# A two-layer hybrid block on one core: two modulation chunks change engine and place, and the rotation is written in half as many products

## The chip, the cores and the metric

The kernel runs on one core of one Trainium2 chip. The metric is device time in microseconds (us) of one execution. The engines are named as in the profile: PE (TensorE, matmuls), DVE (VectorE), ACT (ScalarE), POOL (GpSimd) and SP (SyncE, whose queue issues most transfers).

## What is computed

Two layers over 512 latent tokens and 256 context tokens, width 1024, all in fp32. The parts of the reference that matter here are the modulation vectors, which scale, shift and gate each layer, and the rotation of queries and keys by their grid position:

```python
mod   = (silu(c)     @ mod_w[i] + mod_b[i])     # 6 * 1024 values for the latent tokens
mod_c = (silu(c_ctx) @ mod_w[i] + mod_b[i])     # the same for the context tokens
sh_m, sc_m, g_m, sh_f, sc_f, g_f = split(mod, 6)
h  = rms_norm(x, norm_attn_w[i]) * (1 + sc_m) + sh_m
...                                             # three groups of heads, each its own mixer
x  = x + g_m * (concat([ya, yb, yg]) @ w_out[i])
hf = rms_norm(x, norm_ffn_w[i]) * (1 + sc_f) + sh_f
x  = x + g_f * swiglu(hf, ...)
...
def rotate(xh, pos):                            # on each half of a head, for q and k
    x1, x2 = split(xh, 2)
    return xh * cos + concat([-x2, x1]) * sin
```

## The kernel before

Each fp32 product is made of three passes on PE: weights and activations are split into a high and a low part (`wh`, `wl` for weights), and high x high, high x low and low x high are accumulated. So every weight is loaded into a buffer of the tag `wr` (two buffers), copied to `wh` by ACT (L336) and subtracted to `wl` by DVE (L337). `load_wo` loads a quarter-megabyte piece of the output projection in this way.

The 6 x 1024 modulation values of a layer are made in 12 chunks of 512 weight columns, numbered c = 0 to 11. A chunk is four steps of the generator `mod_dots` (L220); a step takes 128 output columns and multiplies the 1024 x 128 weights, laid out with the columns on the partitions, by the two conditioning rows. These stand in four tiles of 128x512 made by `mod_rows` (L206): two of tag `XFB`, one `YO`, one `HD`, each loaded, passed through tanh on ACT (L214), combined on DVE (L215) and scaled on ACT (L216). A step has four dot products of length 512 in each partition. There are two ways to do them. With `aside` true, each half of the weights is loaded into a slot of tag `QN` (L232, 256 KB), GpSimd multiplies (L239) and ScalarE accumulates (L240). With `aside` false, one load of 512 KB goes into a `wr` buffer (L227) and VectorE multiplies and accumulates in one instruction (L242, listed as CUSTOM_DVE in the profile and as ISA by the compiled program). `step_md(n)` advances the running generator by n steps.

In the first layer, chunks 4 to 9 are made beside the input projections, the convolution of the state-space heads and the start of the attention (about 70 to 264 us), all with `aside`. Chunks 10 and 11 of that layer and all twelve of the next are made with VectorE beside the first layer's feed-forward part, at about 540 to 1070 us. Chunks 4 and 5 are the gate of the attention part's residual (used by `residual`, L1149), 8 and 9 are the scale of the feed-forward norm, first used after the output projection (`sc2`).

The convolution runs in blocks of 128 channels on DVE (L773, L780) and ACT (L768, L778) between PE's projections, and its results are transposed by PE (L796). The scan's decay rows come in by loads named `crow` (L908), and are combined on ACT (L913) and DVE (L917). The rotation is in `head_out` (L672): GpSimd makes x * cos, VectorE makes the swapped halves times sin in eight products of 128x64 (L696), then adds them (L697).

The output projection of the first layer runs as 16 blocks: in the loop over `dA` the first four head tiles for each of eight output pieces (blocks 0 to 7), in a second loop the other four for six pieces (8 to 13), and in its tail for the last two. Each block is one `load_wo`, 24 matmuls (`proj_ws`), and a `residual` on DVE. The code gives only the data flow: a scheduler that works ahead of time with a model of durations writes the order of instructions of every engine and queue, and the tile pools assign buffers in that order. An engine runs its list strictly in that order, waiting where it must; so does SP's queue.

## Time and profile before

| | us |
|---|---|
| three runs | 1818.57, 1820.86, 1827.93 |
| median | 1820.86 |
| the profiled execution, its own time | 1828.21 |
| its span | 1826.4 |

The profiled execution is 7.35 us above the median of the runs. The profile's times are microseconds from the start of the span, unless marked ns. PE is busy for 95% of the span, DVE for 58%, ACT for 37%, POOL for 22%; PEclk is the granted clock of TensorE as a share of full speed, whose two levels are 1.2 and 2.4 GHz. In a row of a timeline, the bracket at the end is the time that the engine sat idle before the instruction and what ended that.

### The profile page before, as it was taken

The numbers are of one execution on the slowest core, as the hardware profiler recorded it, in microseconds if no ns is written. First come the engines' busy times: TensorE is split into PE (matmuls) and PEld (weight loads), VectorE is DVE, ScalarE is ACT, GpSimd is POOL, SyncE is SP. The second block draws the span as 40 slices with busy tenths as digits, with TensorE's granted clock in tenths as the row PEclk, the third lists the DMA queues.
The fourth block names the chain that finished last, engine by engine and source line by source line (L and its number), as shares of the span: only waits on it lengthen the run. The fifth ranks groups of instructions, "written<-read, shape, count | busy, mean of one in ns | idle before, by whom it ended". The sixth has DMA issues, their size and how long they took to land.

```text
span 1826.4 us, 26611 instructions
## 1 busy us (share of the span) xinstructions
PE 1733.7 (95%) x10146; PEld 1475.2 (81%) x10146; DVE 1066.0 (58%) x2165; ACT 682.7 (37%) x1376; POOL 399.6 (22%) x429
## 2 busy tenths in 40 slices
PE   7998897899999999999999989998899999999998
PEld 3887785777878888888888878987777888888887
DVE  4659776886575455445554575576686743333334
ACT  4655664556253211121122234334555532222222
POOL 0398875643020000000000010421552100000000
PEclk9999998999989999999999999999899999999999
DMA  9643655422224343333344455233522333333332
GB/s 363 218 145 112 203 153 150 121 87 67 64 70 127 116 126 108 123 103 109 124 118 120 124 159 186 82 115 110 151 72 65 99 93 92 104 93 94 102 106 79
DMA packets 94319, 221.66 MB, mean 121 GB/s; under 512 B 18416, under 2 KB 26224, under 8 KB 94192
## 3 DMA queue, kind: packets, MB, share of 16 engines
q1 hardware_dynamic: 78096, 204.65, 36.6%
q10 hardware_dynamic: 16096, 15.31, 2.5%
q8 instruction: 80, 1.31, 0.3%
q14 instruction: 47, 0.39, 0.1%
HBM read 198.49 MB, written 21.43 MB: 120 GB/s over the span
## 4 chain that ended last, share of the span: by engine, by line
PE 77%; DVE 9%; DMA 6%; ACT 4%; issue 2%; POOL 2%; SPq 0%; ACTq 0%; DVEq 0%; POOLq 0%
PE S L348 60%; PE sm L446 3%; DMA wl<-crow 2%; PE PT L434 2%; PE PT L348 1%; PE PT L362 1%; PE sm L362 1%; DMA wr<-in_mod_wT_dram 1%; PE S L400 1%; PE sm L938 1%; PE sm L939 1%; PE PT L983 1%; DVE MB L773 1%; PE PT L996 1%; DVE wl L337 1%
## 5 line engine op out<-in xcount | busy, mean ns | idle before, releaser
L336 ACT ACTIVATE wh<-wr 128x1024 fp32r<-128x1024 f32 (+2 forms) x204 | 198.0, 972 | 723.8 <-PE S L348 550.7
L337 DVE TENSOR_TENSOR wl<-wr,wh 128x1024 fp32r<-128x1024 f32 (+2 forms) x204 | 231.2, 1134 | 178.9 <-ACT wh L336 177.0
L280 POOL TENSOR_TENSOR tiny<-tiny,mhalf 128x2 f32<-128x2 f32 (+2 forms) x17 | 28.7, 1689 | 1066.4 <-DVE tiny L1195 1018.7
L348 PE MATMUL S<-HY,wh 128*128 128x512 f32 (+1 forms) x716 | 215.8, 359 | 5.6 <-ACT HY L329 4.0
L348 PE MATMUL S<-HZ,wh 128*128 128x512 f32 (+1 forms) x716 | 213.4, 356 | 1.0 <-DVE HZ L330 1.0
L348 PE MATMUL S<-HS,wh 128*128 128x512 f32 (+1 forms) x716 | 213.0, 355 | 0.0
L348 PE MATMUL S<-HY,wl 128*128 128x512 f32 (+1 forms) x716 | 212.8, 355 | 0.1
L348 PE MATMUL S<-HS,wl 128*128 128x512 f32 (+1 forms) x716 | 209.7, 351 | 0.0
L242 DVE CUSTOM_DVE_ANT_0 PT<-wr,XFB 128x512 f32<-128x512 f32 x112 | 75.6, 716 | 185.6 <-DMA wr<-in_mod_wT_dram 185.5
L348 PEld LDWEIGHTS S<-HY,wh 128*128 128x128 f32 x716 | 118.6, 191 | 24.5 <-ACT HY L329 4.2
L348 PEld LDWEIGHTS S<-HZ,wh 128*128 128x128 f32 x716 | 119.5, 192 | 23.0 <-DVE HZ L330 2.8
L348 PEld LDWEIGHTS S<-HY,wl 128*128 128x128 f32 x716 | 118.8, 192 | 19.5 <-DVE wl L337 0.4
L348 PEld LDWEIGHTS S<-HS,wh 128*128 128x128 f32 x716 | 117.9, 190 | 18.2
L348 PEld LDWEIGHTS S<-HS,wl 128*128 128x128 f32 x716 | 116.6, 189 | 19.0
L348 PE MATMUL S<-PHA,wh 128*128 128x512 f32 (+1 forms) x358 | 105.8, 353 | 0.0
L348 PE MATMUL S<-PHB,wh 128*128 128x512 f32 (+1 forms) x358 | 104.5, 350 | 0.0
L348 PE MATMUL S<-GX,wh 128*128 128x512 f32 (+1 forms) x400 | 97.7, 350 | 0.4 <-DVE KA L1149 0.4
L425 POOL TENSOR_SCALAR pr<-pr,tiny 128x640 f32<-128x640 f32 (+2 forms) x80 | 67.8, 851 | 90.3 <-DVE tiny L424 66.1
L239 POOL TENSOR_TENSOR KA<-QN,XFB 128x512 f32<-128x512 f32 x48 | 68.5, 1430 | 40.8 <-ACT XFB L216 23.1
L434 PE MATMUL PT<-c,pr 128*128 128x128 f32 x384 | 65.0, 286 | 12.8 <-POOL pr L425 5.7
L1296 DVE TENSOR_TENSOR MB<-S,MA 128x768 f32<-128x768 f32 (+1 forms) x42 | 34.6, 823 | 70.7 <-PE S L348 70.7
L348 PEld LDWEIGHTS S<-GX,wh 128*128 128x128 f32 x400 | 65.9, 189 | 11.3 <-DVE KA L1149 0.8
(432 smaller groups left out, 3901.2 us busy)
## 6 DMA issues: line engine op xcount, KB each, us to landing
wr<-in_mod_wT_dram SPq DMA_DIRECT2D x56, 512.0 KB, 3.9
wr<-in_w_gate_dram SPq DMA_DIRECT2D x44, 512.0 KB, 3.6
wr<-in_w_up_dram SPq DMA_DIRECT2D x44, 512.0 KB, 3.6
wr<-in_w_blk_dram SPq DMA_DIRECT2D x28, 512.0 KB, 3.8
wr<-in_w_down_dram SPq DMA_DIRECT2D x32, 448.0 KB, 3.4
QN<-in_mod_wT_dram SPq DMA_DIRECT2D x48, 256.0 KB, 3.0
wr<-in_w_out_dram SPq DMA_DIRECT2D x32, 256.0 KB, 2.7
wr<-in_w_down_dram SPq DMA_DIRECT2D x16, 512.0 KB, 3.5
```

The costliest lines, as they stand in the source:

```text
L239: G.tensor_tensor(out=p_, in0=wv, in1=x, op=ALU.mult)
L242: V.tensor_tensor_reduce(out=p_, in0=wv, in1=x, scale=1.0, scalar=0.0, op0=ALU.mult, op1=ALU.add, accum_out=acc[:, o : o + 1],)
L280: POW.tensor_tensor(out=y, in0=v, in1=mhalf[:, 0:n], op=ALU.pow)
L336: S.activation(hi, raw, AF.Copy)
L337: V.tensor_tensor(lo, raw, hi.bitcast(F32), ALU.subtract)
L348: ins = PE.matmul(pt[:, c0:c1], lhsT=w, rhs=xx[:, c0:c1], start=(k == (0 if len(order) == 1 else order[0]) and i == 0), stop=(k == (nk - 1 ...
L362: PE.matmul(pt[:, 0:n], lhsT=s, rhs=w[:, o : o + n], start=(k == 0 and i == 0), stop=(k == KB - 1 and i == 2),)
L400: PE.matmul(st[:, o0:512], lhsT=Q[:, q0 : q0 + P], rhs=K[:, xk[0] : xk[1]], start=(i == 0), stop=(i == 1))
L425: G.tensor_scalar(out=p_, in0=p_, scalar1=m[:, 4:5], scalar2=1.0, op0=ALU.mult, op1=ALU.mult)
L434: PE.transpose(pt[:, k * P : (k + 1) * P], pr[j, qi][:, kk * P : (kk + 1) * P], ident)
L446: PE.matmul(pv[64 * j : 64 * j + 64, 0:P], lhsT=V2(kts[k], j), rhs=ph[j, qi][:, k, :], start=(k == 0), stop=(k == nkt - 1), tile_position= ...
L1296: V.tensor_tensor(gg[:, c0:c1], pu[:, c0:c1], sg[:, c0:c1], ALU.mult)
```

## The change

Chunks 8 and 9 leave the generator of the first layer's early part. They are made instead with `aside` false in the output projection of that layer: `mod_rows` is called there at the first block, and a step is taken after each of the blocks 2 to 7 of the first loop and each of the first two of the second loop: eight steps. The `mod_rows` at the start of the feed-forward part goes; it uses the same four tiles. The rows are all loaded through the two buffers of tag `MA` instead of `MA` and `MB` in turn, and the sums of a chunk get a tile of their own (`macc`, one buffer). The rotation does the two heads of a tile in one product: four products of 128x128 in place of eight of 128x64.

```diff
@@ -209,7 +209,7 @@
         r = []
         for i, tag in enumerate(("XFB", "XFB", "YO", "HD")):
             t = T(sb, tag, BUFS[tag], [P, 512])
-            x = (ma, mb)[i % 2]([P, 512])
+            x = ma([P, 512])
             nc.sync.dma_start(x, a["cvec"][:, i * 512 : i * 512 + 512].to_broadcast([P, 512]))
             S.activation(t, x, AF.Tanh, scale=0.5)
             V.scalar_tensor_tensor(t, t, 1.0, x, ALU.add, ALU.mult)
@@ -219,7 +219,7 @@
 
     def mod_dots(l, c, rows, ptile, aside):
 
-        acc = tiny(16)
+        acc = T(sb, "macc", 1, [P, 16])
         for b in range(4):
             src = a["mod_wT"][l, 4 * c + b]
             if not aside:
@@ -559,7 +559,7 @@
             rows = mod_rows()
             md = (
                 0
-                for c in range(4, 10)
+                for c in range(4, 8)
                 for _ in mod_dots(
                     0, c, rows, lambda: slot("KA")[:, 0:512], True
                 )
@@ -688,12 +688,11 @@
                     in1=cb, op=ALU.mult,
                 )
             sv = sinT.rearrange("p t (f s c) -> p t f s c", f=2, s=2)
-            for h in range(2):
-                x5 = raw[:, 0:4, 64 * h : 64 * h + 64].rearrange("p t (f s c) -> p t f s c", f=2, s=2)
-                o5 = s[:, :, 64 * h : 64 * h + 64].rearrange("p t (f s c) -> p t f s c", f=2, s=2)
-                for f in range(2):
-                    for k in range(2):
-                        V.tensor_tensor(o5[:, :, f, k, :], x5[:, :, f, 1 - k, :], sv[:, :, f, k, :], ALU.mult)
+            x6, o6 = (z.rearrange("p t (h f s c) -> p t h f s c", f=2, s=2, c=16) for z in (raw[:, 0:4, :], s))
+            for f in range(2):
+                for k in range(2):
+                    sb4 = sv[:, :, f, k, :].unsqueeze(2).to_broadcast([P, 4, 2, 16])
+                    V.tensor_tensor(o6[:, :, :, f, k, :], x6[:, :, :, f, 1 - k, :], sb4, ALU.mult)
             V.tensor_tensor(c, c, s, ALU.add)
             rb = r[:, 12 * i : 12 * i + 12].rearrange("p (t h) -> p t h", h=2).unsqueeze(3)
             V.tensor_tensor(v4(raw[:, 0:4, :]), v4(c), rb[:, 0:4].to_broadcast([P, 4, 2, 64]), ALU.mult)
@@ -1217,10 +1216,14 @@
 
         for i, d in enumerate(dA):
             events(nu + i)
+            if not last and i == 0:
+                rows = mod_rows()
+                md = (0 for c in (8, 9) for _ in mod_dots(0, c, rows, ps_t, False))
             w = load_wo(d, 0)
             pt = ps_s()
             proj_ws(pt, w[0], w[1], [yh[k] for k in WK[0:4]], [yl[k] for k in WK[0:4]], 4, osegs)
             residual(d, pt, 2, parts(ntok), False)
+            step_md(int(i > 1))
             events(nu + i + 0.5)
         events(1e9)
         ysh, ysl_ = [yh[k] for k in WK[4:8]], [yl[k] for k in WK[4:8]]
@@ -1229,6 +1232,9 @@
             pt = ps_s()
             proj_ws(pt, w[0], w[1], ysh, ysl_, 4, osegs)
             residual(d, pt, 2, parts(ntok), True)
+            step_md(1)
+        for _ in md:
+            pass
         sc2 = scale_tiles(l, 4, nfw[l])
         hs2 = []
 
@@ -1262,7 +1268,6 @@
         fw = []
         md = iter(())
         if not last:
-            rows = mod_rows()
             md = (
                 0
                 for z in [(0, 10), (0, 11)] + [(1, c) for c in range(12)]
```

Since lines move by one, L1149 of before is L1148 of after, L780 is L779, and so on. The order of instructions changes at these places.

DVE in the output projection, before: `QN`, `KB` with L1149 are residuals of blocks (S is the block's accumulator), L337 makes the low part `wl` of a later block's weights.

```order
L1149 SCALAR_TENSOR_TENSOR KB_902_4416<-S_1051_5005,mod0_4_732,KB_902_4416 128x512
L337 TENSOR_TENSOR wl_1070_5129<-wr_1068_5126,wh_1069_5128 128x512
...
L1149 SCALAR_TENSOR_TENSOR QN_904_4418<-S_1059_5052,mod0_5_857,QN_904_4418 128x512
L337 TENSOR_TENSOR wl_1074_5162<-wr_1072_5159,wh_1073_5161 128x512
...
L1149 SCALAR_TENSOR_TENSOR QN_905_4419<-S_1067_5099,mod0_5_857,QN_905_4419 128x512
L337 TENSOR_TENSOR wl_1078_5195<-wr_1076_5192,wh_1077_5194 128x512
```

After, on DVE at the same place: PT<-wr with `macc` and L242 is the first dot product of a step, the row with HD its last. The first row is the residual of block 3; `wl_1051` belongs to block 4, whose residual has S_1052, and `wl_1058` to block 5.

```order
L1148 SCALAR_TENSOR_TENSOR QN_871_4287<-S_1045_5000,mod0_5_857,QN_871_4287 128x512
...
L242 ISA PT_1036_4974,macc_1034_4971<-wr_1035_4972,XFB_1006_4820 128x512
...
L242 ISA wr_1035_4972,macc_1034_4971<-wr_1035_4972,HD_1012_4838 128x512
...
L242 ISA PT_1047_5029,macc_1034_4971<-wr_1046_5027,XFB_1006_4820 128x512
...
L242 ISA wr_1046_5027,macc_1034_4971<-wr_1046_5027,HD_1012_4838 128x512
...
L337 TENSOR_TENSOR wl_1051_5038<-wr_1049_5035,wh_1050_5037 128x512
L242 ISA PT_1054_5070,macc_1034_4971<-wr_1053_5068,XFB_1006_4820 128x512
...
L242 ISA wr_1053_5068,macc_1034_4971<-wr_1053_5068,HD_1012_4838 128x512
...
L337 TENSOR_TENSOR wl_1058_5079<-wr_1056_5076,wh_1057_5078 128x512
L1148 SCALAR_TENSOR_TENSOR KA_867_4283<-S_1052_5041,mod0_4_732,KA_867_4283 128x512
```

Before, the `wl` of block 4 (`wl_1070`) stood behind the residual of block 1; after, `wl_1051` stands behind the residual of block 3 and two steps of dot products, and from there on each `wl` stands behind one more step. The pattern goes on up to the eighth step, behind which stands the `wl` of block 10.

SP's queue in the output projection, before:

```order
L334 DMA wr_1080_5225<-in_w_out_dram 128x512
L334 DMA wr_1084_5258<-in_w_out_dram 128x512
L334 DMA wr_1089_5293<-in_w_out_dram 128x512
L334 DMA wr_1094_5329<-in_w_out_dram 128x512
L334 DMA wr_1099_5365<-in_w_out_dram 128x512
L334 DMA wr_1104_5401<-in_w_out_dram 128x512
```

After:

```order
L227 DMA wr_1046_5027<-in_mod_wT_dram 128x1024
L334 DMA wr_1049_5035<-in_w_out_dram 128x512
L227 DMA wr_1053_5068<-in_mod_wT_dram 128x1024
L334 DMA wr_1056_5076<-in_w_out_dram 128x512
L227 DMA wr_1060_5109<-in_mod_wT_dram 128x1024
L334 DMA wr_1063_5120<-in_w_out_dram 128x512
L227 DMA wr_1068_5154<-in_mod_wT_dram 128x1024
L334 DMA wr_1071_5162<-in_w_out_dram 128x512
```

Loads of weights followed each other; now each is followed by a load of a modulation step. Both take the tag `wr` and its two buffers: by the addresses, all steps from the second on go to one of them and all weights from block 4 on to the other, the first step's buffer being that of the weights of block 4.

DVE at the first convolution block, before (L780 is the part of the gate on which PE's transposes wait, L282 to L285 the square root's steps, L699 and L701 the rotated heads):

```order
L282 SCALAR_TENSOR_TENSOR tiny36_372_1748<-tiny36_371_1746 128x36
L283 TENSOR_TENSOR tiny36_372_1748<-tiny36_372_1748,tiny36_370_1744 128x36
L285 SCALAR_TENSOR_TENSOR tiny36_373_1751<-tiny36_372_1748,tiny36_371_1746 128x36
...
L699 TENSOR_TENSOR GR_282_1206<-pr_381_1853,tiny36_373_1751 128x512
L701 TENSOR_TENSOR GR_282_1206<-GR_282_1206,tiny36_373_1751 128x256
L701 TENSOR_TENSOR GR_283_1207<-GR_283_1207,tiny36_373_1751 128x256
L701 TENSOR_TENSOR GR_284_1208<-GR_284_1208,tiny36_373_1751 128x256
L780 SCALAR_TENSOR_TENSOR MB_378_1809<-S_377_1759,MB_378_1809 128x512
```

After:

```order
L282 SCALAR_TENSOR_TENSOR tiny36_338_1628<-tiny36_337_1626 128x36
L779 SCALAR_TENSOR_TENSOR MB_344_1689<-S_343_1639,MB_344_1689 128x512
L283 TENSOR_TENSOR tiny36_338_1628<-tiny36_338_1628,tiny36_336_1624 128x36
...
L285 SCALAR_TENSOR_TENSOR tiny36_339_1631<-tiny36_338_1628,tiny36_337_1626 128x36
...
L698 TENSOR_TENSOR GR_282_1206<-pr_347_1733,tiny36_339_1631 128x512
L700 TENSOR_TENSOR GR_282_1206<-GR_282_1206,tiny36_339_1631 128x256
L698 TENSOR_TENSOR GR_283_1207<-pr_360_1885,tiny36_339_1631 128x512
```

L779 of after (L780 of before) has moved ahead of the norms and the rotated heads. On POOL the last L239 is instruction 105 of its list instead of 143, and on SP's queue the eight steps' 16 loads into `QN` ahead of the attention's `nq` and `crow` loads are gone.

## Rows read from the trace of the kernel before

**Rows 1.** The page, part 1: busy us of each engine, share, instructions.

```profile
PE 1733.7 (95%) x10146; PEld 1475.2 (81%) x10146; DVE 1066.0 (58%) x2165; ACT 682.7 (37%) x1376; POOL 399.6 (22%) x429
```

**Rows 2.** Windows: busy us (xcount) of PE, PEld, DVE, ACT, POOL; PEclk, DMA share, GB/s.

```profile
160.00:170.00 10.00, 5.64 (x48) 5.44 (x46) 9.90 (x12) 2.69 (x7) 9.34 (x8) 0.93 0.30 99
...
190.00:200.00 10.00, 5.14 (x27) 4.40 (x27) 8.85 (x13) 4.91 (x13) 5.79 (x5) 0.80 0.17 52
...
260.00:270.00 10.00, 7.57 (x36) 6.38 (x36) 5.63 (x11) 3.76 (x10) 4.32 (x6) 0.83 0.99 237
...
270.00:280.00 10.00, 5.62 (x38) 5.06 (x36) 7.63 (x18) 6.04 (x15) 7.14 (x12) 0.89 0.74 229
...
280.00:290.00 10.00, 6.30 (x25) 4.61 (x24) 8.23 (x23) 3.64 (x10) 3.11 (x3) 0.59 0.34 100
...
470.00:480.00 10.00, 10.00 (x59) 8.73 (x58) 4.81 (x9) 1.77 (x3) 0.00 (x0) 1.00 0.18 53
```

**Rows 3.** Timeline of PE (start, us, engine line op, [idle before <-releaser]).

```profile
170.72 0.90 PE L796 MATMUL PT<-c,MB 128*128 128x128 f32 x3 [5.08 <-DVE MB L780]
...
198.27 0.90 PE L796 MATMUL PT<-c,MB 128*128 128x128 f32 x3 [4.86 <-DVE zt L815]
...
278.64 0.69 PE L400 MATMUL S<-KA,QN 128*128 128x384 f32 x1 [4.38 <-ACT pr L420]
```

**Rows 4.** Instruction groups by line, 60 to 440 us, shapes apart.

```profile
L239 POOL TENSOR_TENSOR KA<-QN,XFB 128x512 f32<-128x512 f32 x48 | 68.5, 1430 | 40.8 <-ACT XFB L216 23.1 <-DMA QN<-in_mod_wT_dram 7.6 <-ACT KA L240 6.3
...
L240 ACT ACTIVATE KA<-KA 128x512 f32<-128x512 f32 x48 | 30.2, 629 | 8.0 <-POOL KA L239 6.8 <-DVE zt L815 0.6 <-ACT QN L240 0.4
...
L696 DVE TENSOR_TENSOR pr<-GR,c 128x64 f32<-128x64 f32 x24 | 15.1, 694 | 3.3 <-DMA gq<-pr 3.0 <-POOL GR L680 0.3
```

**Rows 5.** Timeline of DVE beside the convolution.

```profile
153.62 1.23 DVE L696 TENSOR_TENSOR pr<-GR,c 128x64 f32<-128x64 f32 x8
...
166.85 3.21 DVE L701 TENSOR_TENSOR GR<-GR,tiny 128x256 f32<-128x256 f32 x3
...
185.63 7.37 DVE L696 TENSOR_TENSOR pr<-GR,c 128x64 f32<-128x64 f32 x8 [2.98 <-DMA gq<-pr]
...
210.00 1.25 DVE L248 TENSOR_TENSOR tiny<-tiny 128x8 f32<-128x8 f32 x1
...
244.25 8.55 DVE L917 SCALAR_TENSOR_TENSOR wh<-wh,dtr,wl 128x128 f32<-128x128 f32 x2
...
264.03 0.31 DVE L248 TENSOR_TENSOR tiny<-tiny 128x8 f32<-128x8 f32 x1
```

**Rows 6.** Timeline of POOL: the end of the 64th L239.

```profile
204.95 1.28 POOL L239 TENSOR_TENSOR QN<-QN,HD 128x512 f32<-128x512 f32 x1
```

**Rows 7.** Timeline of SP's queue: issue, with the time that it stood.

```profile
243.14 12.74 SPq L232 DMA_DIRECT2D QN<-in_mod_wT_dram  x3
...
263.45 0.54 SPq L908 DMA_DIRECT2D wl<-crow  x1
```

**Rows 8.** Timeline of ACT: the decay rows of the scan.

```profile
276.54 1.28 ACT L913 ACTIVATE wl<-wl,dtr 128x128 f32<-128x128 f32 x4 [2.27 <-DMA wl<-crow]
```

**Rows 9.** Timeline of DVE in the output projection.

```profile
461.15 1.14 DVE L1149 SCALAR_TENSOR_TENSOR QN<-S,mod,QN 128x512 f32<-128x512 f32 x2 [0.77 <-PE S L348]
...
465.98 1.14 DVE L1149 SCALAR_TENSOR_TENSOR KA<-S,mod,KA 128x512 f32<-128x512 f32 x2 [0.42 <-PE S L348]
...
470.23 1.14 DVE L1149 SCALAR_TENSOR_TENSOR KB<-S,mod,KB 128x512 f32<-128x512 f32 x2 [2.51 <-PE S L348]
```

**Rows 10.** Source L242 (duration ns min/median/max) and source L227 (its loads).

```profile
L242 DVE CUSTOM_DVE_ANT_0 PT<-wr,XFB x112: 691/702/734, 553.0 to 1066.7; 128x512 f32<-128x512 f32 x112
...
DMA to landing us min/median/max: 3.4/3.9/4.8
```

**Rows 11.** PE timeline at 86 us; DMA issues 60 to 110 us.

```profile
86.49 0.76 PE L348 MATMUL S<-HY,wh 128*128 128x512 f32 x2 [1.33 <-DVE MB L294]
...
MA<-in_cvec_dram SPq DMA_DIRECT2D x2, 256.0 KB, 6.0
```

## The prediction

> **What bounds the kernel now.** I first read the busy time of the engines: PE 95%, DVE 58%, ACT 37%, POOL 22% [rows 1]. Then I read windows of 10 us for where PE is not busy. In the output projection PE has 10.00 of 10 us, DVE 4.81, ACT 1.77 and POOL nothing [rows 2]. PE alone is the bound there, and what is added to the other engines is free until it makes PE wait. Beside the convolution it is the other way round: PE has 5.64 of 10 us at 160 to 170 us with DVE at 9.90 and POOL at 9.34, 5.14 at 190 to 200, and 7.57, 5.62 and 6.30 in the three windows from 260 to 290 [rows 2]. Together 19.7 us of these five windows are idle on PE, and the granted clock is below full in all of them (0.93, 0.80, 0.83, 0.89, 0.59, a mean over the two levels 1.2 and 2.4 GHz). So the change takes work from a stage where the side engines set the pace and puts work into one where PE sets it. Third, I read what ended PE's long idle times: a convolution instruction of DVE (5.08 and 4.86 us) and an exponential of ACT (4.38 us) [rows 3].
>
> **What it takes away beside the convolution.** Two chunks are 32 products of 1.43 us on POOL and 32 accumulations of 0.63 us on ACT [rows 4], with 16 loads on SP's queue. POOL and ACT are not the bound by themselves. What matters is whom they hold up, in three places.
>
> *160 to 170 us.* DVE did its rotated heads, three of them in 3.21 us [rows 5], before the L780 for which PE sat idle 5.08 us [rows 3]. In the order after, that instruction stands before them (and before L283 and L285). Of the 4.36 us that PE lacks in this window I take 3: DVE is busy for 9.90 us in any case, so what is passed must be done soon after, before the next convolution block. Bounds 1 and 4.4.
>
> *190 to 200 us.* Eight products L696 took 7.37 us while POOL multiplied, and eight took 1.23 us at 153.62, when it did not [rows 5]. The delay goes with the number of instructions and not with their size: L248, with eight elements in a partition, took 1.25 us at 210.00 and 0.31 at 264.03 [rows 5]. Four products in place of eight should then take half, 3.7 us less, out of a gap of 4.86 us on PE [rows 3]. Bounds: nothing if the delay goes with size, 4.9 if they meet less of POOL.
>
> *250 to 290 us.* With 64 products instead of 96, POOL has done its last one at about 206 us [rows 6]; the last third ran from there to 263 us. Two L917 took 8.55 us at 244.25 beside them [rows 5], at 128 elements each. SP's queue stood for 12.74 us at 243.14 with loads for these products, and the loads of the decay rows (263.45) were behind that [rows 7]; ACT waited 2.27 us for the last of these at 276.54 [rows 8], ahead of the exponential that ended PE's 4.38 us [rows 3]. PE lacks 10.5 us in 260 to 290 [rows 2]. All of these waits fall away, but the chain through decay rows, scores and softmax stays and will now be the late one. I take 9. Bounds: 4.7 (the 2.27 and the 2.4 that PE lacks at 260 to 270), 10.5.
>
> The Trainium skill bears on this ("SBUF — State Buffer", section "SBUF: two separate sides"): VectorE with two inputs from SBUF and GpSimd take one port pair by an exclusive lock, and the loser is blocked for one whole instruction of the other. By that rule two L917 would lose at most two products. The row says more than that (8.55 us, six products long), so the trace agrees that they exclude each other and not on how long; this sum goes by the row.
>
> The clock: in a window with mean clock x, a share 2(1 - x) ran at the lower level, and half of the matmul time there is what it cost. That is 0.4, 1.0, 1.3, 0.6 and 2.6 us in the five windows, 5.9 in all. With the gaps shorter I take 2 of it back (0 to 4). Sum for this stage: 3 + 3.7 + 9 + 2 = 17.7 us less (bounds 6 and 24). In the second layer the rotation meets no POOL products and DVE is off the path: nothing.
>
> **What it adds in the output projection.** A step is four L242 of about 0.70 us [rows 10], 2.6 us with the sums' readout. PE's period for a block is 4.25 us (465.98 to 470.23), and DVE waits for PE 2.51 us in each [rows 9]. By busy time alone DVE would have 0.7 (`wl`, priced as L242 of the same size) + 1.14 (residual) + 2.6 = 4.4 us per 4.25 us block: nearly free. But a step also waits for its load, and the order puts the `wl` of a block behind it. The load takes 3.4 to 4.8 us, median 3.9 [rows 10], and it can't start before the step before it has released the buffer, since all steps from the second on share one.
>
> Let T be the end of block 3 on PE (461.15 in the trace before [rows 9]). DVE then does the residual (1.14), two evictions of y (L297, priced as the residual: 1.14), and step one until T + 4.8; two more L297 until T + 5.9; step two until T + 8.5; then `wl` of block 4 until T + 9.2. PE starts block 4 on its `wh` and needs `wl` 0.7 us later, so it starts at T + 8.4 where it would have started at T + 0.7, after six transposes of y: 7.7 us late. From here step, load and step follow each other. The third step's load starts at T + 8.5. I take 3.7 us for it, between the shortest and the median, since the traffic here is less than in the feed-forward part, where these were measured. It is done at T + 14.8, and block 5 starts at about T + 14.7 instead of T + 4.9: 9.8 us late. Each further step costs 3.7 + 2.6 = 6.3 us against a block of 4.25, 2.05 us more, five times, up to block 10: 20.1 us. The first long gap and those of about 2 us after it will lower the clock, but PE has slack against the loads until the last of them: 1 us. So 21 us more. With a landing of 3.4 us it is 18.3 + 0 = 18.3, with 4.8 it is 26.6. Bounds 18 and 27.
>
> **Smaller things.** `mod_rows` in the tail of the attention is eight ACT instructions like L240 of 0.63 us [rows 4] and four on DVE like L242: 5.0 and 2.8 us, between other work, and on SP's queue the load of block 3's weights stands behind the rows' loads, which wait for `MA`: 1 us taken (0 to 7.8). The same work taken from the feed-forward start lay under a full PE: 0. At the start the third conditioning row must now wait for the first to be used, as both use `MA`, and such a load takes 6.0 us [rows 11]; the write-back L293 then stands behind it on ACT, and PE already waits 1.33 us for its buffer at 86.49 [rows 11]. I take 2 us (0 to 6).
>
> **Sum.** 1828.2 - 17.7 + 21 + 1 + 2 = 1834.5 us for an execution like the profiled one. That one was 7.35 us above the median of the runs shown, so I set the time at 1827.
>
> **Rivals.** *The loads are hidden.* If the steps find their weights ready, DVE's 4.4 us against 4.25 costs 2 us in all, and the gain stays: 1827 - 21 + 2 = 1808 us. For it: before, loads were issued as soon as a buffer was free, and DMA is busy only a fifth of the time here [rows 2]. Against it: one buffer serves all steps, and landing alone is almost a block long. It decides if landing were below 4.25 - 2.6 = 1.7 us, half of the shortest seen.
>
> *The convolution gives little back, and the stall comes* (the slower side). PE's waits at 250 to 290 us may belong to the chain of the attention itself, with DVE at 8.23 of 10 us in 280 to 290 [rows 2] after POOL's products had ended. Then only the lower bound, 6, is gained: 1827 + 11.7 = 1839 us. For it: 3.7 us are missing in 280 to 290, 17 us and more after the last product. Against it: SP's 12.74 us of standing, which delayed all of that. It decides when the gain is below 12.
>
> *One lock per instruction.* If VectorE loses one GpSimd product per instruction, the two L917 lost 2.9 and not 8 us by it, something else held the rest, and the third place gives 4 instead of 9: 1832 us. The L917 row speaks against it.
>
> **Chances and range.** 0.5% is 9.1 us, about what a measurement of this kernel can tell from no change, so the bounds of "same" are 1811.8 and 1830.0. Forecast 0.58, its own range 1814 to 1840; loads hidden 0.14; little gain 0.23; one lock 0.05. Faster: 0.12 of the hidden case and 0.02 of the forecast: 0.14. Slower: 0.21 of little gain, 0.03 of the lock and 0.13 of the forecast, whose centre is only 3 us below the bound: 0.37. Same: 0.49. The range from 1808 to 1842 leaves out the better half of the hidden case and the worse part of little gain, together under 0.2.
>
> **What would show it.** In the profile after: PE idle for about 8 us before block 4 of the output projection and 2 us before each of blocks 5 to 10, ended by DVE `wl` L337, with DVE idle before L242 on the load; that stage 21 us longer. Beside the convolution: no L239 after about 206 us, no L917 above 1 us, the idle times at 170, 198 and 278 us short, and the output projection's start some 15 us earlier. The prediction is wrong if steps find their weights ready, if PE's idle time before 445 us stays as it is, or if the start of the kernel loses more than 6 us.

## The result, and the profile after

The changed kernel takes 1848.69 us (median of four runs, 1840.30 to 1852.78). The kernel before took 1822.48 on the same chip (four runs, 1818.57 to 1827.93). The ratio is 1.0136, with a 95% interval from 1.009 to 1.0182: slower, by 26 us between the medians. The profiled execution took 1852.78 us, the longest of the four.

First the page of the kernel after: the busy line of part 1, and of part 2 the slices of PE, POOL and the granted clock.

```profile
PE 1747.1 (94%) x10146; PEld 1485.0 (80%) x10146; DVE 1070.7 (58%) x2205; ACT 663.5 (36%) x1312; POOL 351.8 (19%) x397
...
PE   7998897899789999999999999999899999999998
...
POOL 0397515552010000000000002231553000000000
PEclk9989898999889999999999999999899999999999
```

PE is busy for 13 us more than in [rows 1]. POOL is busy for 48 us less, about the 32 products of 1.43 us that left it [rows 4]. Where the 24.6 us between the two spans went is read by setting the starts of the same PE and DVE instructions side by side (lines of the kernel after stand one lower from the rotation on: L695 is L696 of before).

| start of an instruction | before, us | after, us | grown by, since the row above |
|---|---|---|---|
| L597 in the second stage of the start | 107.50 | 114.29 | 6.8 |
| convolution: L796 behind PE's wait for `zt` | 198.27 | 208.68 | 3.6 |
| first score matmul L400 | 270.42 | 272.61 | -8.2 |
| first residual of the output projection | 450.55 | 453.27 | 0.5 |
| first norm matmul L306 behind it | 516.80 | 541.48 | 22.0 |

Of the first 6.8, 3.3 are there before 69 us, in work that the change doesn't touch. The experiment with the same start (own_buffers, below) doesn't have them, and run 7 has 1.7: this part varies between executions. The middle of the kernel gave 4.6 us from 114 to 272. The output projection then took 22.0.

**The start and the convolution.** The timeline of PE after, its waits there.

```profile
91.74 0.98 PE L348 MATMUL S<-HY,wh 128*128 128x512 f32 x2 [3.83 <-DVE MB L294]
...
176.48 0.66 PE L707 MATMUL sm<-c,GR 128*128 128x128 f32 x2 [2.62 <-DVE GR L700]
...
185.17 0.55 PE L795 MATMUL PT<-c,MB 128*128 128x128 f32 x3 [3.00 <-ACT GX L801]
...
208.68 0.90 PE L795 MATMUL PT<-c,MB 128*128 128x128 f32 x3 [4.87 <-DVE zt L814]
```

The wait at 91.74 was 1.33 us at 86.49 [rows 11]. The 5.08 at 170.72 [rows 3] is gone, but 2.62 and 3.00 have come behind it, and the wait for `zt`, 4.86 at 198.27 [rows 3], is as long as it was and 10 us later.

**The output projection.** The timeline of PE after, from the transposes of y to block 7 of the weights.

```profile
466.93 1.52 PE L1044 MATMUL PT<-c,HY 128*128 128x128 f32 x6 [2.39 <-DVE macc L242]
472.17 1.65 PE L348 MATMUL S<-GR,wh 128*128 128x512 f32 x4 [3.71 <-ACT wh L336]
...
478.57 0.85 PE L348 MATMUL S<-GR,wh 128*128 128x512 f32 x4
...
483.71 0.98 PE L348 MATMUL S<-GR,wh 128*128 128x512 f32 x4 [0.59 <-ACT wh L336]
...
490.76 0.96 PE L348 MATMUL S<-GR,wh 128*128 128x512 f32 x4 [1.45 <-ACT wh L336]
```

The timeline of DVE after, over the same stretch: a residual, `wl` of blocks 4 and 5, and the first L242 of two steps.

```profile
463.93 1.14 DVE L1148 SCALAR_TENSOR_TENSOR QN<-S,mod,QN 128x512 f32<-128x512 f32 x2 [1.52 <-PE S L348]
...
472.15 0.69 DVE L337 TENSOR_TENSOR wl<-wr,wh 128x512 fp32r<-128x512 f32 x1
476.09 0.70 DVE L242 CUSTOM_DVE_ANT_0 PT<-wr,XFB 128x512 f32<-128x512 f32 x1 [3.25 <-DMA wr<-in_mod_wT_dram]
...
478.58 0.69 DVE L337 TENSOR_TENSOR wl<-wr,wh 128x512 fp32r<-128x512 f32 x1
...
482.34 0.70 DVE L242 CUSTOM_DVE_ANT_0 PT<-wr,XFB 128x512 f32<-128x512 f32 x1 [2.01 <-DMA wr<-in_mod_wT_dram]
```

The `wl` at 472.15, of block 4, comes after two steps of four L242, and from 476.09 on the first L242 of each step waits for its load (3.25 us, then 2.01). The L242 that begin a step stand at 476.09, 482.34, 488.66, 495.11, 501.19 and 507.46: a period of 6.27 us. In windows of 20 us this is (columns as in [rows 2]):

```profile
460.00:480.00 20.00, 13.90 (x68) 11.46 (x67) 14.14 (x37) 4.53 (x8) 0.00 (x0) 0.74 0.18 54
480.00:500.00 20.00, 15.23 (x79) 11.86 (x78) 13.34 (x37) 1.89 (x3) 0.00 (x0) 1.00 0.38 133
```

Before, [rows 2] show 10.00 us of 10 for PE in this stage. Now 6.1 us are missing in the first 20 and 4.8 in the second, while DVE isn't full either: both wait for loads. SP's queue after shows why the weights of block 4 are late too:

```profile
468.63 0.33 SPq L334 DMA_DIRECT2D wr<-in_w_out_dram  x1
```

The load of block 4's weights is issued at 468.63, right behind the last L242 of step one, whose buffer it takes; `wh` is made of it just ahead of 472.17, where PE starts block 4. The loads of the third step (472.24) and of the next weights (472.87) follow the end of step two in the same way.

### The profile page after: what moved, and what is told of

Read it like the earlier page. It is cut to its first block, busy times and chain, and to the rows that moved or that the text cites. A ratio compares the mean times of both kernels' runs of the same rounds, so it can differ in the third digit from the quotient of the medians.

```text
span 1851.0 us, 26522 instructions
## 1 busy us (share of the span) xinstructions
PE 1747.1 (94%) x10146; PEld 1485.0 (80%) x10146; DVE 1070.7 (58%) x2205; ACT 663.5 (36%) x1312; POOL 351.8 (19%) x397
## 3 DMA queue, kind: packets, MB, share of 16 engines
HBM read 198.49 MB, written 21.43 MB: 119 GB/s over the span
## 4 chain that ended last, share of the span: by engine, by line
PE 79%; DVE 8%; DMA 7%; ACT 3%; issue 2%; POOL 1%; SPq 0%; ACTq 0%; POOLq 0%; DVEq 0%
PE S L348 60%; PE sm L446 3%; PE PT L362 3%; DMA wr<-in_mod_wT_dram 2%; DMA wl<-crow 2%; PE sm L362 2%; PE PT L434 2%; PE PT L348 1%; PE S L400 1%; PE PT L982 1%; PE sm L938 1%; DVE PT L242 1%; PE sm L937 1%; DVE wl L337 1%; PE S L189 1%
## 5 line engine op out<-in xcount | busy, mean ns | idle before, releaser
L337 DVE TENSOR_TENSOR wl<-wr,wh 128x1024 fp32r<-128x1024 f32 (+2 forms) x204 | 230.2, 1129 | 187.0 <-ACT wh L336 184.8
L242 DVE CUSTOM_DVE_ANT_0 PT<-wr,XFB 128x512 f32<-128x512 f32 x128 | 86.4, 716 | 199.3 <-DMA wr<-in_mod_wT_dram 199.2
L348 PEld LDWEIGHTS S<-HS,wl 128*128 128x128 f32 x716 | 117.5, 190 | 18.3
L1148 DVE SCALAR_TENSOR_TENSOR QN<-S,mod,QN 128x512 f32<-128x512 f32 (+1 forms) x64 | 39.0, 631 | 51.1 <-PE S L348 51.1
```

What stands on the lines that cost most here:

```text
L242: V.tensor_tensor_reduce(out=p_, in0=wv, in1=x, scale=1.0, scalar=0.0, op0=ALU.mult, op1=ALU.add, accum_out=acc[:, o : o + 1],)
L337: V.tensor_tensor(lo, raw, hi.bitcast(F32), ALU.subtract)
L348: ins = PE.matmul(pt[:, c0:c1], lhsT=w, rhs=xx[:, c0:c1], start=(k == (0 if len(order) == 1 else order[0]) and i == 0), stop=(k == (nk - 1 ...
L1148: V.scalar_tensor_tensor(xT[d][:, c0:c1], pt[:, c0:c1], mod_ap(l, which, d, v), xT[d][:, c0:c1], ALU.mult, ALU.add)
```

## The experiments

Each ratio is to the kernel before, run on the same chip. The median of before was 1825.6 us beside the first four runs, 1824.8 beside the next four, 1829.6 beside the next four and 1831.6 beside the last three, so ratios compare across groups better than times do.

**1. Own buffers for the late steps.** The kernel after, with the weights of chunks 8 and 9 in the tag `vh` in place of `wr`, which the output projection's own weights use too.

```
-                md = (0 for c in (8, 9) for _ in mod_dots(0, c, rows, ps_t, False))
+                md = (0 for c in (8, 9) for _ in mod_dots(0, c, rows, ps_t, False, "vh"))
```

> The changed kernel with one difference: the eight steps in the output projection load into the two buffers of tag vh, which is idle there, instead of sharing the two of tag wr with the weights. Theory (the stall is the load of a step that can't start before the step before it has freed the shared buffer, with the next weights' low part queued behind it on VectorE): the 22 us that the output projection lost come back but for 2 to 4, so about 1827 to 1831 where the changed kernel has 1848.7. Rival (VectorE's 4.4 us of work against a block of 4.25, or the traffic of 768 KB per block, sets the pace): 1843 or more.

1829.2 us, 1.0011 [0.9995, 1.0026]. The output projection took 66.8 us (before 66.25, after 88.2). The timeline of DVE:

```profile
468.92 1.14 DVE L1148 SCALAR_TENSOR_TENSOR KA<-S,mod,KA 128x512 f32<-128x512 f32 x2
469.98 0.68 DVE L337 TENSOR_TENSOR wl<-wr,wh 128x512 fp32r<-128x512 f32 x1
...
473.10 1.14 DVE L1148 SCALAR_TENSOR_TENSOR KB<-S,mod,KB 128x512 f32<-128x512 f32 x2 [1.22 <-PE S L348]
474.16 0.68 DVE L337 TENSOR_TENSOR wl<-wr,wh 128x512 fp32r<-128x512 f32 x1
...
475.81 0.69 DVE L242 CUSTOM_DVE_ANT_0 PT<-vh,XFB 128x512 f32<-128x512 f32 x1
```

The same four L242 are there; only now no step in this stage waits for a load, and the residual waits for PE, as in [rows 9]. The stall was the shared buffer, and with it goes nearly the whole loss. But no gain is left either.

**2. The late steps left out.** The kernel after with chunks 8 and 9 set to their bias.

> The changed kernel with chunks 8 and 9 left out altogether (their modulation is the bias alone, so the scale of the first layer's feed-forward norm is another), and the conditioning rows made at the feed-forward part as in the kernel before: no step in the output projection, and none beside the convolution. Theory (the stage before the output projection gained only what stands in the trace, some 8 us at 208 to 272 us, and lost as much before that): within 4 us of the kernel before, 1819 to 1827. Rival, the prediction's own term (17.7 us less beside the convolution, 2 lost at the start): 1806 to 1808.

1822.34 us, 0.9971 [0.9952, 0.9991]. With nothing added in the output projection, the kernel is 5 us faster by the ratio and not the 15.7 of the prediction (17.7 less the 2 at the start, which this run keeps): most of the gain at the convolution isn't there. Its profile gains 5.6 us from the second L597 to the first score matmul, and the norm behind the output projection starts 0.7 us earlier than before (516.09). That profile also runs the feed-forward part, from 576 to 1053 us of before, 9.0 us faster than before, where the other profiles stay within 3.1 us of before. Why isn't known, so not all of the 5 us need be the change's.

**3. The rotation alone.** The kernel before with the new rotation.

> The kernel before with the rotation in four products of 128x128 instead of eight of 128x64, and nothing else. Theory (beside GpSimd's products a VectorE product with two SBUF inputs is held until GpSimd pauses, whatever their number): no change, within 2 us of the kernel before, and the products at about 190 us still take 6 to 8 us. Rival (each product is held for about one of GpSimd's): the four take 3.7 us, and the kernel gains 3 to 4 us.

1822.07 us, 0.9989 [0.9973, 1.0005]. Half as many products bring nothing that can be measured, though the interval still holds the 3.7 us of the prediction. The expectation that the products at 190 us still take 6 to 8 us failed. The timeline of DVE there:

```profile
187.78 4.58 DVE L695 TENSOR_TENSOR pr<-GR,c 128x128 f32<-128x128 f32 x4 [3.11 <-DMA gq<-pr]
...
192.46 1.60 DVE L696 TENSOR_TENSOR pr<-pr,pr 128x512 f32<-128x512 f32 x1
```

The four took 4.58 us, where eight took 7.37 before [rows 5], and PE's wait for `zt` fell to 2.83. But the products began 2.15 us later than before, the addition L696 behind them met GpSimd in turn (1.60; 0.69 before), and PE's wait for `zt` ended at 198.49 (before 198.27). In another place, at 121.85, one of the twelve took 6.41 us by itself.

**4. The rows through two buffers at the start.** The kernel after, in which the first `mod_rows` loads through `MA` and `MB` in turn, as before.

```
-            x = ma([P, 512])
+            x = (tags or (ma, ma))[i % 2]([P, 512])
...
-            rows = mod_rows()
+            rows = mod_rows((ma, mb))
```

> The changed kernel with the conditioning rows of the first call loaded through MA and MB in turn, as before; those of the second call in the output projection still through MA. Theory (with MA alone the third row waits for the first, and the write-back of the keys behind it makes PE wait 3.8 instead of 1.3 us at about 90 us, with 1.5 us more after it): 2 to 4 us less than the changed kernel, 1845 to 1847, and the idle time before PE's matmul at about 90 us back to 1.3 us. Rival (the wait is hidden by later ones): no change, 1848 to 1850.

1845.86 us, 1.0092 [1.0064, 1.0119]. PE's wait for the write-back is 1.32 us again, at 88.17, and the second L597 starts at 107.61 as before (107.50).

**5. The last third left out.** The kernel *before* without chunks 8 and 9: the most that moving them can give.

> The kernel before with chunks 8 and 9 left out (their modulation is the bias alone), and nothing else changed: old rotation, rows through MA and MB, the last third of GpSimd's products gone from beside the convolution. It is the change's first half by itself. Theory (taking the last third away moves the wait to the next chain before the scores start, and gives 2 to 6 us): 1817 to 1822 where the kernel before has 1823 to 1825. Rival (the prediction's sum for the places at 250 to 290 us and 160 to 170 us holds when nothing else is changed, 9 and 3 and the clock's 2): 1809 to 1812.

1822.85 us, 0.9990 [0.9977, 1.0004]. The scores start 3.8 us earlier. A single L696, at 122.52, took 7.58 us.

**6. All six chunks left out.** The kernel before with nothing of the modulation beside the convolution.

> The kernel before with all six chunks left out that GpSimd makes beside the projections and the convolution (4 to 9, their modulation is the bias alone), with their conditioning rows and loads. It bounds from above what any such move can give. Theory A (the products that remain in the changed kernel, two thirds of them, hold VectorE at 120 to 205 us, and are where the expected gain is still lost): 15 to 25 us less than before, 1800 to 1810. Theory B (the stage is bound by the convolution's own chain on VectorE and ScalarE): 10 us less at most, 1814 or more.

1795.1 us, 0.9846 [0.9826, 0.9866]: 28 us less by the ratio. Its window from 125 to 215 us (columns as in [rows 2]):

```profile
125.00:215.00 90.00, 89.07 (x615) 82.19 (x614) 56.68 (x113) 30.82 (x59) 22.35 (x26) 1.00 0.30 100
```

The same window of the kernel after:

```profile
125.00:215.00 90.00, 78.86 (x524) 72.84 (x524) 72.63 (x114) 46.13 (x133) 68.87 (x65) 0.92 0.39 120
```

The same window of the kernel before:

```profile
125.00:215.00 90.00, 77.46 (x516) 71.21 (x516) 77.27 (x124) 49.26 (x139) 77.86 (x69) 0.92 0.42 135
```

PE lacks 0.9 us of 90 without any chunk, 11.1 in the kernel after and 12.5 in the kernel before (the windows are the same in time, not to the matmul in work). So the stage is held by the 64 products that the change leaves in their place, and hardly by the 32 that it takes away.

**7. Both repairs (1 and 4).**

> The changed kernel with both repairs: the steps of the output projection in the buffers of tag vh, and the first call's rows through MA and MB. Theory (the two add): 2 to 4 us less than with the buffers alone (1829.2), so 1825 to 1828, and no better than the kernel before by more than 2 us. Rival (the gain beside the convolution shows once nothing eats it): 1812 to 1818.

1826.15 us, 1.0015 [1.0003, 1.0027]. The change without its two faults changes the time by less than 0.3%.

**8. Two more chunks late.** As 7, with chunks 6 and 7 in the output projection too, a step in each block.

> As the kernel with both repairs, but chunks 6 and 7 go from GpSimd to the output projection as well: 16 steps there, one after each block, and only 32 products left beside the convolution. The steps need 2.6 us of VectorE in each of 16 blocks of 4.25 us, beside 1.8 to 2.8 of its own. Theory (VectorE is then full: the stage gets longer by 5 to 10 us, and the stage before it gains 5 to 10): 1820 to 1832. Rival (freed of two thirds of the products, the convolution gains 15 or more): 1808 to 1815, better than both kernels.

1820.86 us, 0.9980 [0.9969, 0.9992]. The scores start at 245.94 (24.5 us earlier), but the output projection takes 74.3 us, 8 more, the norm behind it waits 4.12 us for the last chunk, and up to 576 us another 7.5 us are lost.

**9. Chunks 6 and 7 behind a pause.** As 7, but GpSimd gets them only behind a one-column copy of the fourth convolution block.

```
+            if not last and b == 3:
+                mark = G.tensor_copy(out=tiny(1), in_=xb[b][:, 0:1]).ins
+                with tc.issue_after(mark):
+                    step_md(8)
```

Not shown here: the calls that took these steps further ahead are removed.

> The kernel with both repairs, in which GpSimd's products of chunks 6 and 7 are issued behind a one-column copy that GpSimd makes of the fourth convolution block, so that GpSimd is free of products from about 130 us until that block is done; chunks 8 and 9 stay in the output projection with buffers of their own. Theory (what held the stage are the products that meet VectorE's work at 130 to 205 us; products after that cost little, as leaving out the last third showed): the scores start 12 to 22 us earlier than at 270 us, and the time is 1804 to 1815. Rival (products cost the same wherever they meet VectorE): 1822 to 1828.

1820.86 us, 0.9941 [0.9917, 0.9965]: 11 us less by the ratio; expected were 10 to 21 us less than the 1824.8 of the group ahead. The profiled execution, at 1826.63, is 5.8 us above the median; what follows is what held it back, and faster executions may have had less of it. The convolution's last L796 starts at 249.99 (before 264.17), but the scores wait. The timeline of PE in run 9, at the first scores:

```profile
269.22 0.66 PE L400 MATMUL S<-KA,QN 128*128 128x384 f32 x1 [13.72 <-DMA KA<-nk]
```

That of SP's queue, with the time that each issue stood:

```profile
231.30 9.17 SPq L232 DMA_DIRECT2D QN<-in_mod_wT_dram  x4
...
249.74 14.89 SPq L368 DMA_DIRECT2D QN<-nq  x3
264.80 1.11 SPq L368 DMA_DIRECT2D KA<-nk  x2
```

That of DVE, one L917:

```profile
246.40 14.30 DVE L917 SCALAR_TENSOR_TENSOR wh<-wh,dtr,wl 128x128 f32<-128x128 f32 x1 [1.41 <-ACT wl L913]
```

And that of POOL beside it:

```profile
245.55 1.31 POOL L239 TENSOR_TENSOR QN<-QN,YO 128x512 f32<-128x512 f32 x1
...
255.36 5.19 POOL L945 TENSOR_TENSOR HY<-GX,c 128x256 f32<-128x256 f32 x9
```

One L917 of 128 elements takes 14.30 us, to 260.70, while POOL goes from one instruction to the next up to 260.55. SP's queue stands 14.89 us with three loads of `nq`, ahead of those of the keys, which PE waits for. The two are one chain, as ACT's timeline shows:

```profile
262.18 0.82 ACT L775 ACTIVATE S<-MB 128x772 f32<-128x772 f32 x1 [12.46 <-DVE MB L770]
```

ACT waits for a convolution instruction that stands behind the held L917 on DVE; its sums of the last products (L240) come after that, and the third load of `nq` is issued at 264.19, when one of them has freed its `QN`.

**10 and 11. Which half of a product costs.** The kernel before, in 10 without GpSimd's products of chunks 6 and 7 (ScalarE sums the loaded weights), in 11 without ScalarE's sums of them.

> The kernel before with GpSimd's products of chunks 6 and 7 left out: ScalarE sums up the loaded weights themselves, so loads, buffers and sums stay and those two chunks' modulation values are other ones. Theory (it is GpSimd's products that hold VectorE): 12 to 25 us less than the kernel before, and VectorE busy for much less in 125 to 215 us than 77 us. Rival (the sums on ScalarE or the loads on SP's queue hold the stage): within 5 us of the kernel before.

> The counterpart: the kernel before with ScalarE's sums of chunks 6 and 7 left out and GpSimd's products and loads kept (those two chunks' values are other ones). Theory (products hold VectorE): within 5 us of the kernel before. Rival (the sums take ScalarE's time from the convolution): 12 us less or more.

1818.64 us, 0.9938 [0.9916, 0.9961], and 1833.92 us, 1.0018 [1.0003, 1.0032]. The products cost and the sums don't. Run 10's 11 us are slightly less than the range expected. A likely reason is that the products of chunks 8 and 9 move up into the free place: GpSimd's last product ends at 226.6 (before 263.2), and it is still busy for 65.9 of the 90 us from 125 (before 77.9). The profile of run 10 is of its slowest execution, 1827.02, and doesn't show the gain: this verdict rests on the times.

**12. The pause in the kernel before**, for chunks 6 to 9.

> The kernel before with only the position of the products changed: chunks 6 to 9 all stay on GpSimd, behind the same copy of the fourth convolution block. Theory: the convolution gains as with the pause, but the 32 loads of these chunks then stand ahead of the attention's loads on SP's queue until about 265 to 275 us, so that the scores start at 270 us or later: 1818 to 1830. Rival (position is all that counts): 1804 to 1812.

1848.87 us, 1.0095 [1.0074, 1.0116], a miss. The timeline of PE:

```profile
306.11 0.66 PE L400 MATMUL S<-KA,QN 128*128 128x384 f32 x1 [45.62 <-DMA KA<-nk]
```

The convolution does gain: its last L796 start at 252.97 (before 264.17). But with 64 products that late, the loads of the keys stand behind theirs, and PE waits 45.62 us.

**13 and 14. Products one at a time.** All products of a stage write one tile, so that GpSimd starts each only when ScalarE has summed the one before it. 13 is the kernel before with this, 14 is run 7 with it.

```
-                    x, p_ = rows[2 * v + hf], ptile() if v == 0 else wv
+                    x, p_ = rows[2 * v + hf], ptile() if v == 0 or aside else wv
...
+            kt = slot("KA")[:, 0:512]
...
-                    0, c, rows, lambda: slot("KA")[:, 0:512], True
+                    0, c, rows, lambda: kt, True
```

> The kernel before with one output tile for all of GpSimd's products, so that each product must wait until ScalarE has summed up the one before it (about 0.9 us): the same 96 products, with a pause after each instead of runs without one. Theory (a VectorE instruction with two SBUF inputs gets no turn as long as GpSimd goes from one instruction to the next, so the length of GpSimd's runs is what counts, and one such wait was 14.3 us in the kernel with the pause): no L917 and no L696 above 3 us, though products go on to about 290 us, and 5 to 15 us less than the kernel before. Rival (each product takes its own time from VectorE, pause or not): the same time as before or 5 to 15 us more, since the products last longer.

> The kernel with both repairs (own buffers in the output projection, first rows through two tags), and its 64 early products through one output tile, each waiting for the sum of the one before. Theory of the runs without a pause: the stage at 125 to 215 us gains, 1808 to 1818. Rival: 1824 to 1835.

13: 1878.09 us, 1.0251 [1.0227, 1.0274]. The time expected was missed: no DVE instruction between 60 and 340 us takes over 2 us any more, as expected, and the convolution's last L796 start 10 us earlier (253.78), but 96 products in single file last until 334.8 us, and their loads stand ahead of those of the scores, which PE now lacks:

```profile
322.30 0.66 PE L400 MATMUL S<-KA,QN 128*128 128x384 f32 x1 [60.64 <-DMA QN<-nq]
```

14: 1817.39 us, 0.9918 [0.9901, 0.9935], 14 us less than before in its group and the best of all that keep the whole computation. GpSimd's products end at 255.5 us there (206.5 in run 7). The timeline of POOL in run 14:

```profile
187.63 1.30 POOL L239 TENSOR_TENSOR KA<-QN,YO 128x512 f32<-128x512 f32 x1 [2.73 <-ACT KA L240]
189.76 1.28 POOL L239 TENSOR_TENSOR KA<-QN,XFB 128x512 f32<-128x512 f32 x1 [0.83 <-ACT KA L240]
```

Its source view of L917 (duration in ns, min/median/max, first and last start):

```profile
L917 DVE SCALAR_TENSOR_TENSOR wh<-wh,dtr,wl x12: 337/352/749, 236.1 to 265.8; 128x128 f32<-128x128 f32 x12
```

Its window, to set beside that of the kernel after in 6:

```profile
125.00:215.00 90.00, 80.55 (x541) 74.39 (x541) 68.35 (x113) 46.85 (x118) 63.38 (x56) 0.92 0.43 141
```

Where one product directly follows another, POOL waits 0.83 us or more for ScalarE. No L917 beside the products takes longer than 0.75 us, no DVE instruction between 60 and 340 us longer than 2, and PE has 1.7 us more of the 90 (3.7 more than in run 7, 76.85). The scores start at 257.05, 10.8 us earlier than in run 7 (267.86). The edit also spreads the products over 49 us more and no longer writes any over the loaded weights, so how much of the gain is due to the pauses alone isn't shown.

**15. One chunk behind a pause, three late.**

> The kernel with the pause, but only chunk 6 is made by GpSimd behind the fourth convolution block, and chunk 7 goes to the output projection (12 steps there), so that SP's queue has 8 loads instead of 16 ahead of the attention's. Theory (the pause gained its 15 to 20 us by 250 us and lost them to the wait of the scores for their keys' loads, 13.7 us): the scores start at 250 to 257 us, the output projection takes 3 to 6 us longer, 1806 to 1814. Rival (something else holds the scores to 268 us): 1820 to 1828.

1821.36 us, 0.9936 [0.9915, 0.9958], above the range expected. The scores start at 252.28 as expected, but the output projection with 12 steps takes 73.9 us, 7.6 more than before, and its norm waits 6.10 us.

## Why the prediction was wrong

The time lies outside the range, above it. Every term of loss stayed within its bounds, the start once the 3.3 us that vary are taken off; the gain did not. For an execution like the profiled one the prediction had 6.3 us more than before (1834.5 against 1828.2); the two profiles differ by 24.6. Of the 18.3 us between, 13.1 are the missing gain, 4.8 the start and 1.0 the output projection, less about 0.5 in the attention's tail.

**The output projection: right in size, and half of the path.** Predicted 21 us more, with block 4 at T + 8.4, block 5 at T + 14.7 and 6.3 us per step after. Measured 22.0, with T at 463.93: block 4 at T + 8.24 (the text's own terms, added up again, give 8.6 in place of 8.4), block 5 (PE, 478.57) at T + 14.64, 6.27 per step. PE wasn't idle for 8 us at a stretch, as the text had it, but twice, 2.39 and 3.71 us, with the transposes of y between, and at a lower clock (0.74 in the window). The wait before block 4 was ended by `wh` and not by `wl`: its weights were loaded late, since step one had their buffer. `wl` behind two steps would have let PE start at the same time (472.84 less 0.7), so it is in part luck that this number agrees so well. From block 6 on PE waits for both (0.45 to 1.45 us for `wh`, up to 0.88 for `wl`). The 2.51 us that DVE was said to wait in each block before are in one of the three [rows 9], but nothing hung on them. Run 1 shows the cause: the same work from a buffer of its own costs 0.6 us in this stage.

**The start: right.** Predicted 2 us. PE waits 2.50 us more for the write-back (3.83 in place of 1.33), and run 4 takes this wait away. Of the 6.8 us by the second L597, 3.5 came behind 69 us; run 1, with the same start, comes there 2.2 us later than before. The 6.8 would pass the 6 us that the prediction named as a sign of being wrong, but only by the part that varies. The attention's tail (predicted 1) is in the 0.5 us of the table.

**The gain of 17.7 us beside the convolution: this step failed.** From 114 to 272 us the profile after gained 4.6, run 7 gained 3.0 and run 5, with chunks 8 and 9 gone altogether, 5.1 (from the second L597 to the first score matmul, each against before).

*160 to 170 us, 3 us:* PE doesn't wait at L796 for L780 in the profile after, but it came to that stretch 6.8 us late. In run 7, which starts as before does, the same wait is 7.33 us and longer than before (5.08). The order of DVE's work changed, the amount did not, and GpSimd's 64 products stand beside it as they did.

*190 to 200 us, 3.7 us:* "the delay goes with the number of instructions" was read from eight L696 in 7.37 us [rows 5], and these eight bear it out. The source view of L696 before (columns as in run 14):

```profile
L696 DVE TENSOR_TENSOR pr<-GR,c x21: 211/285/1573, 124.3 to 192.8; 128x64 f32<-128x64 f32 x21
```

The timeline of POOL before, at the end of these eight:

```profile
191.44 1.30 POOL L239 TENSOR_TENSOR QN<-QN,YO 128x512 f32<-128x512 f32 x1
194.88 1.82 POOL L239 TENSOR_TENSOR KA<-QN,XFB 128x512 f32<-128x512 f32 x1 [2.14 <-ACT KA L240]
```

No single one takes over 1.57 us, about one GpSimd instruction. Runs 3, 4 and 7 bear it out as well: there the four took 4.58, 5.07 and 5.23 us, none over 1.62. That is 2.1 to 2.8 us less than the eight had taken, and still PE came no sooner to the transposes behind `zt` (198.49, 200.12 and 199.70; before 198.27). But what the rows ahead of the prediction hid, since they put several instructions in one, is the other form of the same delay. The timeline of DVE after, the first of four products:

```profile
195.37 7.25 DVE L695 TENSOR_TENSOR pr<-GR,c 128x128 f32<-128x128 f32 x1 [3.41 <-DMA gq<-pr]
```

The timeline of POOL after, beside it:

```profile
194.30 1.70 POOL L686 TENSOR_TENSOR pr<-GR,c 128x128 f32<-128x128 f32 x4
...
201.19 1.28 POOL L239 TENSOR_TENSOR QN<-QN,HD 128x512 f32<-128x512 f32 x1
205.29 1.82 POOL L239 TENSOR_TENSOR KA<-QN,XFB 128x512 f32<-128x512 f32 x1 [2.82 <-ACT KA L240]
```

One of four products takes 7.25 us, past six GpSimd instructions. In both kernels it is over when POOL pauses: in before POOL's run ends at 192.74 and the eighth L696 follows at 192.75; after, the run ends at 202.47 and the product at 202.62. In this form the length is set by how long GpSimd goes on, and not by the number or the size of the products: one of 128x128 took 6.41 us at 121.85 in run 3, one of 128x64 took 7.58 at 122.52 in run 5. So the term fails by this delay in the profile after, and in the runs without it by what is saved not reaching PE.

*250 to 290 us, 9 us:* here the profile after did gain, 8.2 us from the `zt` wait to the scores (run 7 gains 4.0, run 5 6.3). The last L239 ends at 209.58 and no L917 up to 300 us takes more than 0.80, as predicted; PE's waits of 1.51 and 2.43 us at 257 and 264 are gone. The wait at the softmax, 4.38 us [rows 3], is 3.48 at 279.88: most of it belongs to the chain of the attention. And the two L917 in 8.55 us [rows 5] were no two delays. The timeline of DVE before, cut so that the first L917 stands alone:

```profile
242.98 1.02 DVE L773 SCALAR_TENSOR_TENSOR MB<-S,c,MB 128x771 f32<-128x771 f32 x1
243.92 0.41 DVE L815 SCALAR_TENSOR_TENSOR zt<-zt,PT 128x256 f32<-128x256 f32 x1
244.25 8.29 DVE L917 SCALAR_TENSOR_TENSOR wh<-wh,dtr,wl 128x128 f32<-128x128 f32 x1
```

The timeline of POOL before, beside it:

```profile
242.30 1.29 POOL L239 TENSOR_TENSOR KA<-QN,XFB 128x512 f32<-128x512 f32 x1
...
251.09 1.29 POOL L239 TENSOR_TENSOR QN<-QN,HD 128x512 f32<-128x512 f32 x1
```

One L917 takes 8.29 us, to 252.54; POOL's run ends at 252.38.

Beside the size of the terms, their sum was wrong in kind: the kernel's pace here is set by the first 64 products, which the change leaves where they were. Run 6 (28 us for all six chunks) against run 5 (2 us for the last two) shows it, and run 10 that it is GpSimd's part of them. Runs 9 and 12, which move products behind the fourth block, and runs 13 and 14, which put pauses between them, all end the convolution 10 us earlier or more. What of the 28 us can be had without dropping work stays open: run 14 has half, runs 8 and 15 reach the scores 24.5 and 18.1 us earlier than before and lose much of it again behind them, and run 9's profile loses at the scores the 14 us that it won in the convolution. What decides between the two forms of the delay wasn't tried either.

**The rivals.** "Little gain, and the stall" (1839 us) was the mechanism, for another reason than the one given there: not the attention's own chain alone, but GpSimd's remaining products. The measured time is still 10 us above it. In the profiles the gain was 1.4 below its 6, the start 4.8 above its term, 3.3 of that by chance, and the output projection 1.0 above; and the profile after lies 4.1 us above its median, where 7.35 had been taken off. "Loads hidden" fell with the first L242 that waited. "One lock per instruction" fell with the 8.29 us.

The Trainium skill ("SBUF — State Buffer", section "SBUF: two separate sides") has the shared pair taken by whichever starts first, for its whole instruction. The eight L696 of before agree (at most 1.57 us each). The 7.25, 8.29 and 14.30 us do not: there the loser let six and more instructions of the other pass. Its remark that operations off the shared pair wait for nobody agrees: L773 and L815, with one input in PSUM, took 1.02 and 0.41 us beside the same products.

## What to carry to other kernels

Before pricing what a move takes away, ask by leaving it out, or by the rows of the stage, whether the part that stays holds the stage by itself; a stage with two thirds of its load left can be as slow as before. Split grouped rows of a timeline into single instructions before making a rule of their mean: "two in 8.55" was one in 8.29. A prefetch that is put into a stage needs buffers that no consumer of that stage shares, and loads that are moved later in a queue delay what is issued behind them.

## What was not expected of the hardware

A VectorE instruction with both inputs in SBUF can be held for as long as GpSimd goes from one such instruction to the next without a pause, 14.30 us for 128 elements in run 9, and ended within 0.16 us of the end of GpSimd's run in the three cases shown. The first 320 us of all the traces hold 21 VectorE instructions of over 3 us. In none of them does GpSimd pause while the instruction is held, and each ends 0.08 to 0.15 us after GpSimd's run, or 1.08 after it where it is a split of weights of 128x1024 (L337 of before). In other places instructions of the same kind got through once per GpSimd instruction. With a pause of 0.83 us or more between directly following products, run 14, the longest L917 beside them was 0.75 us.
